# Hybrid decoder block: warm-up on a tile of ones, the last row's banks filled ahead, and new due times

## The chip, the cores and the metric

One NeuronCore of one Trainium2 chip. The kernel is one program on one core. Times are device microseconds of an execution; the time before is the median of 3 runs. The engines are named as in the profile: PE (TensorE matmuls), PEld (its weight loads), DVE (VectorE), ACT (ScalarE), POOL (GpSimd) and SP (SyncE, which here only issues transfers).

## The reference, cut to what matters

One layer of a decoder trunk on 512 positions of width 1024, in float32, with 97 MB of weights.

```python
h = rmsnorm(x) * g                                # 512 x 1024
proj = h @ w_in                                   # gated conv B, C, v | GLU a, b | queries | 3 gates
y_a = (B * conv3(C * v)) @ w_a_out
y_b = silu(layernorm(conv31(a * sigmoid(b)) + bias)) @ w_b_out
k, vm = split((rmsnorm(mem) * g_mem) @ w_kv)      # 256 memory tokens, 4 heads of 256
y_c = softmax(q k^T / 16) vm @ w_att_out
x = x + (sum of sigmoid(gate_i) * y_i) @ w_o
u = conv3(rmsnorm(x) @ w_up);  gt, up = split(u)  # 2 x 2816
x = x + (silu(gt) * up) @ w_down
return rmsnorm(x) * g_final
```

## The kernel before

**Arithmetic.** Every float32 product is made of three matmuls in a faster format: each operand is split into a high part (a cast, on ACT) and a low part (operand minus high part, on DVE), and high x high, high x low and low x high are added in one PSUM bank. So each weight unit of 128 x 1024 words is loaded by a transfer into `wf`, cast by ACT to `whi` (L638), subtracted by DVE to `wlo` (L642), and then used by 24 matmuls of 256 columns or 12 of 512. The large products are made by a scheme with seven in place of eight block products, which needs sums of blocks of the activations (made by DVE) and of the weights (mostly added by transfers that POOL issues, L762).

**Stages, in order of time.** The keys and values of the memory (`K`, `V`; matmuls at L1093 and, through the helper `product`, L589 to L591), the norm of x, the mixer's input products with the two convolutions and the attention between them (matmuls at L808), the three output products with their gates (L1580 to L1582), `w_o`, the FFN's up products (L808 again) with conv3 taps (L1536), gate product `z` (L1899) and its splits (`zh` L2086, `zl` L2093), and the down product by seven block products called a, b, d, c, f, e, g (L589 to L591 again). In the down product a, c, e and g follow each other in the same two banks ("chain e" is what a, c and e left there).

**Who sets the order.** PE's order is written out by hand (`seq`). All other work is a list of jobs with an engine, a cost, predecessors and places in buffers. `Jobs.run` plays them through with a small model: at each step it takes, over all engines, the job that can start first, and among those that can start at the same time the one with the smallest due. A due is counted back from PE's order, or is the place in the hand-written list `jobs.first` (15 names, places -15 to -1; they cover the first loads), and to it the table `LATER` adds a number for each kind of job. `AHEAD` says how long before its due a kind may start at the earliest; a kind that is not in it may start at once. A kind is the engine and the first words of the job's name (`SP ldm`: loads of the memory tiles). The resulting order is then fixed for each engine.

**The start.** `warm_up` (L1930) multiplies the identity matrix, which POOL builds (a fill and a select), 9 times with itself; float32 products run as two passes, so there are 18 rows. SP loads the memory's transposed tiles in halves of 256 KB (`ldm`, L906) and the first weights of K and V in halves (`ld0`, L1027). ACT makes `mh` (L916), DVE `ml` (L923), ACT and DVE make the halves of `whi` and `wlo` (L1036, L1040). PE's first product is K's first unit by halves (`K0`: 12 matmuls each), then V's first unit by halves (6 matmuls each), then V's second unit and so on.

**The end.** Product g adds to bank t = 0 of the chain for row block 2's left half, and for row block 3's left half it uses two banks of their own, 256 columns each (`end_banks`, `end_steps`), so that the last matmuls of each finish one after the other. Row block 3's left half is therefore its residual, plus what chain e left in bank t = 1 (`read_end(2)`, L2248, before g ends), plus the end banks (`read_end(0)` and `read_end(1)`, L2248, after their last matmul). Then ACT squares each half and sums it (L2251), takes the root (L2272), DVE the reciprocal (L2326), and DVE scales the left half in two parts (`last_scaled`, L2291), ACT the right half (`right_scaled`, L2278). Each part is stored at once: L2280, L2287 and L2294 on SP, the last right half on ACT's queue. Row blocks 0 to 2 go the same way, with L2284 for the left half.

Of the kernel before, what the change touches and what calls it, by code (L numbers as in the profile page):

```python
# [14 lines left out]
P = 128  # L15
# [62 lines left out]
    "ACT c3": 11.82, "ACT cf": -173.01, "ACT csq": -118.38, "ACT exp": -328.94,  # L78
# [3 lines left out]
    "ACT m root": -184.55, "ACT mgh a": -50.41, "ACT mgh b": 12.56, "ACT mgh c": 9.52,  # L82
    "ACT mgh d": 53.07, "ACT mgh e": -17.66, "ACT mgh f": 328.16, "ACT mgh g": -26.95,
    "ACT mh": 113.01, "ACT msq": -103.23, "ACT mu high": -95.05, "ACT oh": -89.08,
# [8 lines left out]
    "ACT sa": 32.95, "ACT sg": 5.87, "ACT sigmoid": 255.67, "ACT silu": -398.77,  # L93
    "ACT sq": -293.17, "ACT sr": -87.26, "ACT swish": -14.1, "ACT tap 0": 43.05,
    "ACT tap 1": 18.01, "ACT tap 2": -228.98, "ACT tap 3": 177.05, "ACT tp 0": -29.48,
# [9 lines left out]
    "ACT xroot": -102.97, "ACT xsq": -103.24, "ACT xsquare": 24.41, "ACT zh a": -216.1,  # L105
    "ACT zh b": -131.07, "ACT zh c": -165.28, "ACT zh d": -50.38, "ACT zh e": -12.01,
    "ACT zh f": -0.17, "ACT zh g": 24.3, "DVE CV": -0.26, "DVE c3": 18.44, "DVE centre": 14.23,
    "DVE cf": 2.06, "DVE csum": 176.43, "DVE ends": 101.48, "DVE fl h b00": -8.47,
# [4 lines left out]
    "DVE hd": -0.61, "DVE kl": -10.74, "DVE kt": 186.09, "DVE lns": -8.31, "DVE low": -452.45,  # L113
    "DVE m fold": -54.18, "DVE m scale": -85.77, "DVE mgl a": -80.95, "DVE mgl b": -52.58,
    "DVE mgl c": -276.12, "DVE mgl d": -6.76, "DVE mgl e": -420.56, "DVE mgl f": -72.56,
    "DVE mgl g": 51.17, "DVE ml": -3.7, "DVE ms c": -29.57, "DVE ms d": -655.28,
    "DVE ms e": -37.35, "DVE ms f": -0.78, "DVE msum": 27.5, "DVE mu fold": -21.28,
    "DVE mu low": -259.6, "DVE mu sum": -65.96, "DVE ol": -72.74, "DVE pn": -7.9,
    "DVE ptl": -14.54, "DVE ql": -83.03, "DVE r2 glu": 917.93, "DVE r2 up": 167.98,
# [5 lines left out]
    "DVE rl": -1.6, "DVE s6 glu": -90.48, "DVE sum": 19.99, "DVE sv": -29.87, "DVE tap 0": -45.34,  # L125
    "DVE tap 1": -70.16, "DVE tap 2": 353.84, "DVE tap 3": 43.8, "DVE top": -52.16,
    "DVE tot1": -14.34, "DVE tot2": 102.84, "DVE um": 102.16, "DVE v scale": -37.68,
    "DVE var fold": 7.3, "DVE var sum": 3.04, "DVE vl": 24.74, "DVE wl K 0": 49.62,
# [9 lines left out]
    "DVE x1 g": 14.24, "DVE xn": -647.51, "DVE xnorm": 196.37, "DVE xsum": -68.7,  # L138
    "DVE ymul": -34.71, "DVE ys": -1.41, "DVE z": -34.43, "DVE zd": 0.07, "DVE zl a": -144.78,
    "DVE zl b": -105.24, "DVE zl c": 218.14, "DVE zl d": 2.42, "DVE zl e": 85.69,  # L140
    "DVE zl f": 17.13, "DVE zl g": -3.75, "DVE zs c": 122.42, "DVE zs d": 21.17,
    "NONE c3": -263.88, "NONE cf": -131.91, "NONE mem tile": -34.72, "NONE raw tile K": 2.19,
    "NONE raw tile V": -2.93, "NONE rows": -101.12, "NONE sums": 33.35, "NONE temps": -19.31,
# [5 lines left out]
    "POOL s7 glu": -196.56, "POOL s7 up": -11.58, "POOL wadd e": 33.74, "POOL wadd x": -2.01,  # L149
    "POOL wadd y": 9.99, "POOL wl merge 0": -341.32, "POOL wl merge 2": 20.27, "POOL xa": -55.62,  # L150
# [308 lines left out]
def hybrid_block_kernel(  # L459
# [1466 lines left out]
    def warm_up():  # L1926

        ps = make(("bank", "warm"))
        for i in range(9):
            nc.tensor.matmul(ps[:, :P], ident, ident, start=True, stop=True)  # L1930
# [470 lines left out]
```

## Time and profile before

| | us |
|---|---|
| median of 3 runs | 897.81 (897.07 to 898.18) |
| the profiled execution | 897.59 |
| its span, first to last instruction | 895.8 |
| PE busy | 885.8 (99%) |
| DVE busy | 823.9 (92%) |
| ACT busy | 677.6 (76%) |

A row of the timeline gives the start and the length of an instruction in us, engine, line, operation, output <- inputs, shapes and count, and in brackets how long the engine idled before it and what ended that. A row of the chain of waits gives start, length and what the end of the program hung on. A row of the table by stretches gives the window, its length, then for PE, PEld, DVE, ACT and POOL the busy time (and instructions), then the granted PE clock, the mean busy share of the 16 DMA engines and GB/s. A matmul's row is longer than the distance to the next one, because matmuls overlap.

### The profile page before, as it was taken

The page shows a single profiled execution, that of the slowest core. Times are in us where ns is not written, and L with a number is a line of the kernel's source. Part 1 is how long each engine was busy: PE and PEld are TensorE (multiplying, and loading weights), DVE is VectorE, ACT ScalarE, POOL GpSimd, SP SyncE. Part 2 cuts the span into 40 slices and gives each one's busy share as a digit, 9 for nine tenths or more (in the row PEclk, how much of TensorE's full clock was granted, in tenths as well). Part 3 has the DMA queues.
Part 4 walks back from the last instruction along what each step waited for, and adds up shares of the span by engine and source line. Part 5 has one row for each costly group of instructions (what it writes and reads, how often), then busy time and mean ns, then how long its engine had stood idle before and what let it go on. Part 6 is the DMA issues. An engine that isn't in the chain of part 4 may idle for free.

```text
span 895.8 us, 16734 instructions
## 1 busy us (share of the span) xinstructions
PE 885.8 (99%) x6657; PEld 848.1 (95%) x6657; DVE 823.9 (92%) x929; ACT 677.6 (76%) x934; POOL 126.7 (14%) x153
## 2 busy tenths in 40 slices
PE   9999999999999999999999999999999999999997
PEld 8999999999989999999899988899999999988886
DVE  6997999999989999999978869898998889999997
ACT  7677989988988879778948743777776677866566
POOL 0011121101011121111100001021121121002120
PEclk9999999999999999999999999999999999999999
DMA  9998788757779889987858488599999878679992
GB/s 357 386 243 181 178 205 190 178 143 164 198 158 240 170 197 223 227 210 194 210 122 273 139 252 198 147 230 308 282 259 218 205 149 167 197 266 302 251 202 94
DMA packets 54366, 190.60 MB, mean 213 GB/s; under 512 B 6160, under 2 KB 6544, under 8 KB 54288
## 3 DMA queue, kind: packets, MB, share of 16 engines
q0 software_dynamic: 20880, 75.24, 46.3%
q1 hardware_dynamic: 33120, 114.02, 36.0%
q8 instruction: 52, 0.85, 0.4%
q10 hardware_dynamic: 288, 0.27, 0.1%
q14 instruction: 26, 0.21, 0.1%
HBM read 185.31 MB, written 4.19 MB: 212 GB/s over the span
## 4 chain that ended last, share of the span: by engine, by line
PE 94%; DVE 2%; ACT 1%; issue 1%; DMA 1%; SPq 0%; DVEq 0%
PE bank L808 60%; PE bank L590 6%; PE bank L591 6%; PE bank L589 6%; PE bank L1580 5%; PE bank L1581 5%; PE bank L1582 5%; PE bank L1093 2%; DVE wlo L642 1%; DMA mem<-in_mem_t 1%; PE bank L1819 0%; PE bank L1333 0%; ACT j L2251 0%; DVE upc L1536 0%; DVE gtc L1536 0%
## 5 line engine op out<-in xcount | busy, mean ns | idle before, releaser
L638 ACT CAST whi<-wf 128x1024 fp32r<-128x1024 f32 (+1 forms) x205 | 212.2, 1040 | 72.3 <-PE bank L808 35.1
L642 DVE TENSOR_TENSOR wlo<-wf,whi 128x1024 fp32r<-128x1024 f32 (+1 forms) x199 | 239.3, 1211 | 26.4 <-ACT whi L638 26.2
L1405 ACT ACTIVATE tp<-u,pk 128x511 f32<-128x511 f32 (+22 forms) x184 | 119.7, 707 | 5.7 <-DVE acc L1412 4.0
L1412 DVE TENSOR_TENSOR acc<-acc,tp 128x1020 f32<-128x1020 f32 (+22 forms) x92 | 109.2, 1189 | 5.6 <-ACT tp L1405 3.8
L762 POOL DMA_DIRECT2D wf<-in_w_in x56 | 49.5, 899 | 255.4 <-DVE wlo L642 170.0
L808 PE MATMUL bank<-ft6h,wlo 128*128 128x256 f32 x232 | 63.9, 275 | 0.7 <-DVE wlo L642 0.7
L808 PE MATMUL bank<-fb10h,whi 128*128 128x256 f32 x232 | 64.0, 276 | 0.0
L808 PE MATMUL bank<-fb11h,whi 128*128 128x256 f32 x232 | 64.0, 276 | 0.0
L808 PE MATMUL bank<-fb00h,whi 128*128 128x256 f32 x232 | 63.9, 275 | 0.0
L808 PE MATMUL bank<-fb00l,whi 128*128 128x256 f32 x232 | 63.8, 275 | 0.0
L808 PE MATMUL bank<-fb00h,wlo 128*128 128x256 f32 x232 | 63.8, 275 | 0.0
L808 PE MATMUL bank<-fb10l,whi 128*128 128x256 f32 x232 | 63.8, 275 | 0.0
L808 PE MATMUL bank<-fb10h,wlo 128*128 128x256 f32 x232 | 63.8, 275 | 0.0
L808 PE MATMUL bank<-ft5l,whi 128*128 128x256 f32 x232 | 63.8, 275 | 0.0
L808 PE MATMUL bank<-ft5h,wlo 128*128 128x256 f32 x232 | 63.8, 275 | 0.0
L808 PE MATMUL bank<-ft6l,whi 128*128 128x256 f32 x232 | 63.8, 275 | 0.0
L808 PE MATMUL bank<-ft7l,whi 128*128 128x256 f32 x232 | 63.8, 275 | 0.0
L808 PE MATMUL bank<-ft7h,wlo 128*128 128x256 f32 x232 | 63.8, 275 | 0.0
L808 PE MATMUL bank<-ft4l,whi 128*128 128x256 f32 x232 | 63.8, 275 | 0.0
L808 PE MATMUL bank<-ft4h,wlo 128*128 128x256 f32 x232 | 63.8, 275 | 0.0
L808 PE MATMUL bank<-fb11l,whi 128*128 128x256 f32 x232 | 63.8, 275 | 0.0
L808 PE MATMUL bank<-fb11h,wlo 128*128 128x256 f32 x232 | 63.8, 275 | 0.0
(381 smaller groups left out, 3143.1 us busy)
## 6 DMA issues: line engine op xcount, KB each, us to landing
wf<-in_w_in POOLq DMA_DIRECT2D x56, 512.0 KB, 6.8
wf<-in_w_in SPq DMA_DIRECT2D x54, 512.0 KB, 5.5
wf<-in_w_up POOLq DMA_DIRECT2D x33, 512.0 KB, 7.3
wf<-in_w_up SPq DMA_DIRECT2D x29, 512.0 KB, 6.8
wf<-in_w_down SPq DMA_DIRECT2D x15, 512.0 KB, 4.5
wf<-in_w_att_out SPq DMA_DIRECT2D x8, 512.0 KB, 3.6
wf<-in_w_a_out SPq DMA_DIRECT2D x8, 512.0 KB, 3.7
wf<-in_w_b_out SPq DMA_DIRECT2D x8, 512.0 KB, 4.6
```

Of the source, the lines that this page charges most:

```text
L589: nc.tensor.matmul(ps, s_hi, w_hi, start=start, stop=False, skip_group_check=again)
L590: nc.tensor.matmul(ps, s_hi, w_lo, start=False, stop=False, skip_group_check=again)
L591: nc.tensor.matmul(ps, s_lo, w_hi, start=False, stop=stop, skip_group_check=again)
L638: nc.scalar.copy(parts[0], src())
L642: nc.vector.tensor_tensor(lo, src(), hi.bitcast(F32), op=ALU.subtract)
L762: nc.gpsimd.dma_start(out=tiles[key], in_=block(w, col[c], k), accum_op=ALU.add)
L808: nc.tensor.matmul(ps[:, c, :], w[:, i, at], in_turns(a[i]), start=first and n == 0, stop=i == 3 and n == 2, skip_group_check=again,)
L1405: nc.scalar.activation(two(("tp", p, s))[:, j, s:], two(("u", p))[:, j, : SEQ - s], AF.Copy, scale=weight(j),)
L1412: nc.vector.tensor_tensor(a, a, two(("tp", p, s))[:, :, s:], op=ALU.add)
L1580: nc.tensor.matmul(ps, w_hi[:, i, at], hi, start=first, stop=False)
L1581: nc.tensor.matmul(ps, w_hi[:, i, at], lo, start=False, stop=False)
L1582: nc.tensor.matmul(ps, w_lo[:, i, at], hi, start=False, stop=last)
```

## The change

Three parts, in one edit.

- `warm_up` multiplies a tile of ones, which DVE fills, 11 times with itself; it waits for that fill and no longer for POOL's identity. In the first K unit the high x high matmuls of its first half (4 of the 12) become a PE job of their own, `K00`, ahead of the other 8. The second chunk of the first `mh` is made by DVE (`first_high`) and no longer by ACT.
- The end banks are filled by DVE before g starts: residual plus what chain e left in bank t = 1, in two adds of 256 columns. g's matmuls are added to that, with no starting flag. The adds after g are gone; ACT squares and DVE scales straight from the banks. g's first PE job waits for the fill.
- `LATER` and `AHEAD` are replaced as a whole (a few hundred numbers; the diff below shows the entries that the text names), and the kinds `sa`, `sv`, `sq`, `hd`, `sr`, `rt` and `rc` of the last rows now have a number for each row block.

```diff
 LATER = {
...
-    "SP ldm": -808.23, "SP ld0 K": -1347.82, "SP ld0 V": -250.98, "SP ld V 0": -0.13,
+    "SP ldm": 1.07, "SP ld0 K": -59.18, "SP ld0 V": 0.74, "SP ld V 0": -0.51,
-    "ACT sa": 32.95, "ACT rt": -228.68, "DVE z": -34.43, "DVE cf": 2.06,
+    "ACT sa 0": -186.83, "ACT rt 1": -69.87, "ACT rt 2": -135.8, "DVE z": 26.85, "DVE cf": 235.06,
...
 }
...
-        elif key[0] in ("tap", "tp"):
+        elif key[0] in ("tap", "tp", "sa", "sv", "sq", "hd", "sr", "rt", "rc"):
             words = key[:2]
...
-                for i in range(2 * e, 2 * e + 2):
+                for i in range(2 * e, 2 * e + (1 if g == e == 0 else 2)):
                     nc.scalar.activation(
                         tiles["mh", g][:, i, :], four(("mem", g))[:, i, :], AF.Copy,
                         scale=par("norm_mem_g", 4 * g + i),
                     )
+
+            def first_high():
+                memory_parts(0)
+                nc.vector.tensor_scalar(
+                    tiles["mh", 0][:, 1, :], four(("mem", 0))[:, 1, :], par("norm_mem_g", 1), None,
+                    op0=ALU.mult,
+                )
...
+            pe(("K00",), 4 * MM_QUAD, lambda: keys_product(0, 0, (0, 1), (0,)),
+               [("wh0", "K", 0), ("mh", 0, 0), "mh1"], take=[(bank, "ps")], unit=False)
             for e in range(2):
-                pe(K0 if e else ("K0",), 12 * MM_QUAD,
-                   lambda e=e: keys_product(0, 0, (2 * e, 2 * e + 1)), [("wl0", "K", e), ("ml", 0, e)],
-                   take=[] if e else [(bank, "ps")], use=[bank] if e else [], unit=e == 1)
+                pe(K0 if e else ("K0",), (12 if e else 8) * MM_QUAD,
+                   lambda e=e: keys_product(
+                       0, 0, (2 * e, 2 * e + 1), (0, 1, 2) if e else (1, 2)),
+                   [("wl0", "K", e), ("ml", 0, e)], use=[bank], unit=e == 1)
...
         ps = make(("bank", "warm"))
-        for i in range(9):
-            nc.tensor.matmul(ps[:, :P], ident, ident, start=True, stop=True)
+        w = tiles["ones",][:, :P]
+        for i in range(11):
+            nc.tensor.matmul(ps[:, :P], w, w, start=True, stop=True)
+
+    def ones():
+        nc.vector.memset(make(("ones",))[:, :P], 1.0)
...
         if p == "g":
-            banks = banks[:1] + (end_banks if u == 1 else [])
+            banks = banks[:1] + (end_banks if u < 2 else [])
+            needs += [("rd", "end")] if u == 0 else []
...
                 product(
-                    ps[:, :256], hi[:, k % 2, cols], lo[:, k % 2, cols],
+                    end_bank(i), hi[:, k % 2, cols], lo[:, k % 2, cols],
                     four(("zh", "g", k // 4))[at], four(("zl", "g", k // 4))[at],
-                    k == 0, k == PAIRS - 1,
+                    False, k == PAIRS - 1, again=True,
                 )
...
-    def read_end(i):
-        row = late["x1"][NT - 1][0]
-        src = tiles["bank", chain("e"), 1]
-        if i < 2:
-            row, src = row[:, ENDS[i]], tiles[end_banks[i]][:, :256]
-        nc.vector.tensor_tensor(parted(row), parted(row), turned(src), op=ALU.add)
+    def read_end():
+        row, src = late["x1"][NT - 1][0], turned(tiles["bank", chain("e"), 1])
+        for i in range(2):
+            make(end_banks[i])
+            nc.vector.tensor_tensor(
+                turned(end_bank(i)), parted(row[:, ENDS[i]]), parted(src[:, i, :]), op=ALU.add)
...
+    def square_end(i, into):
+        nc.scalar.activation(late["junk"][0][:, ENDS[i]], end_bank(i), AF.Square, accum_out=into)
...
         nc.vector.scalar_tensor_tensor(
-            x1, x1, r_fin[NT - 1], late["g"][0][:, cols], op0=ALU.mult, op1=ALU.mult
+            parted(x1), turned(end_bank(i)), r_fin[NT - 1], parted(late["g"][0][:, cols]),
+            op0=ALU.mult, op1=ALU.mult,
         )
...
             job(("sr", t, 1), "ACT", 0.4, lambda: square_end(1, ss_fin[last][:, 0:1]),
                 [("pd", "g", "rest", 1)], use=[end_banks[1]])
```

More of the change, by code (lines that the diff above doesn't have):

```diff
@@ L140 @@
[L140 to L143, printed above, removed]
[5 rows of a table removed]
-    "POOL s7 glu": -196.56, "POOL s7 up": -11.58, "POOL wadd e": 33.74, "POOL wadd x": -2.01,
-    "POOL wadd y": 9.99, "POOL wl merge 0": -341.32, "POOL wl merge 2": 20.27, "POOL xa": -55.62,
[7 rows of a table removed]
+    "ACT c3": -1.33, "ACT cf": -332.1, "ACT csq": 6.48, "ACT exp": 144.98, "ACT fh h b00": 1.04,
[3 rows of a table added]
@@ L158 @@
+    "DVE zl b": -133.2, "DVE zl c": -1.95, "DVE zl d": -57.09, "DVE zl e": -106.84,
+    "DVE zl g": -287.13, "DVE zs c": 331.9, "DVE zs d": -188.27, "DVE zs e": 198.82,
+    "NONE c3": -197.54, "NONE cf": 11.65, "NONE mem tile": -0.5, "NONE raw tile K": 4.49,
+    "NONE raw tile V": -1.04, "NONE sums": 3.7, "NONE temps": -26.39, "POOL ea": 5.97,
[6 rows of a table added]
+    "POOL wadd x": -92.48, "POOL wadd y": -265.13, "POOL wl merge 0": 0.31,
[7 rows of a table added]
 }
 AHEAD = {
-    "ACT cf": 41.7, "ACT csq": 1.4, "ACT exp": 30.8, "ACT fh h b00": 29.2, "ACT fh h b11": 14,
@@ L181 @@
-    "DVE mu fold": 8.3, "DVE mu low": 21.4, "DVE ol": 1.5, "DVE pn": 13.5, "DVE ptl": 1.9,
-    "DVE ql": 1.6, "DVE r3 cv": 6.6, "DVE r3 gate": 25.2, "DVE r3 q": 3.4, "DVE r7 bb": 29.2,
-    "DVE r7 cv": 5.7, "DVE r7 gate": 1.6, "DVE r7 glu": 1.6, "DVE rd c": 26.3, "DVE rd e": 18.2,
-    "DVE rd end": 12.8, "DVE rd f": 60, "DVE rl": 2.8, "DVE s6 glu": 1.2, "DVE tot1": 1.7,
-    "DVE var sum": 120.3, "DVE vl": 1.3, "DVE wl V 0": 114.3, "DVE wl merge 1": 17.6,
[7 rows of a table removed]
-    "NONE cf": 3.5, "NONE mem tile": 2.7, "NONE raw tile K": 39.9, "NONE raw tile V": 1.4,
@@ new lines @@
+    "ACT r1 gate": 34.5, "ACT r1 q": 1.5, "ACT r2 gate": 8.3, "ACT r2 glu": 53.1,
[4 rows of a table added]
+    "ACT sa 0": 1.7, "ACT sa 1": 49, "ACT sg": 1.7, "ACT sigmoid": 44.7, "ACT silu": 1.5,
+    "ACT sq 3": 51.6, "ACT sr 1": 5.2, "ACT sr 2": 3.8, "ACT swish": 86.3, "ACT tap 0": 135,
+    "ACT tap 1": 3.6, "ACT tap 3": 1.3, "ACT v root": 74.6, "ACT vh": 1.5, "ACT wh K 0": 5,
[4 rows of a table added]
+    "ACT zh a": 4.8, "ACT zh d": 17.5, "ACT zh g": 3.3, "DVE csum": 10.8, "DVE ends": 9.1,
[3 rows of a table added]
+    "DVE kl": 42.8, "DVE kt": 52.5, "DVE low": 2.8, "DVE m fold": 3, "DVE m scale": 5.4,
@@ L204 @@
+    "DVE zl a": 65.2, "DVE zl d": 8, "DVE zl e": 85.2, "DVE zl f": 37.3, "DVE zl g": 22.2,
+    "NONE c3": 1.1, "NONE cf": 41.5, "NONE mem tile": 8.1, "NONE raw tile K": 1.9,
+    "NONE raw tile V": 2.5, "NONE rows": 3.9, "NONE sums": 45.8, "POOL s3 cv": 7.1,
[8 rows of a table added]
 }
@@ L901, in hybrid_block_kernel, with memory_parts @@
     R_MEM, R_X, R_V, SS_X, ATT = column(0, MC), column(2, NT), column(60, NT), 6, 12
+    def memory_parts(g):
+        for part, side in (("mh", "h"), ("ml", "l")):
+            if (part, g) not in tiles:
+                tiles[part, g] = forms.tile(
+                    [P, 4, HALF], F32R, tag=MEM_PLACE[g] + side, name=name(part))
     for g in range(2):
@@ L911, in mem_high @@
                 if e == 0:
[L912 to L915 removed]
+                    memory_parts(g)
+                for i in range(2 * e, 2 * e + (1 if g == e == 0 else 2)):
                     nc.scalar.activation(
@@ L1928, in warm_up @@
         ps = make(("bank", "warm"))
-        for i in range(9):
-            nc.tensor.matmul(ps[:, :P], ident, ident, start=True, stop=True)
-    pe(("warm",), 4.9, warm_up, take=[(("bank", "warm"), "ps")], unit=False)
+        w = tiles["ones",][:, :P]
[3 more added lines that the diff above has]
+        nc.vector.memset(make(("ones",))[:, :P], 1.0)
+    job("ones", "DVE", 0.2, ones, take=[(("ones",), ANY)])
+    pe(("warm",), 4.75, warm_up, ["ones"], take=[(("bank", "warm"), "ps")], use=[("ones",)],
+       unit=False)
     KEYS = lambda h, g: lambda: pe_keys(h, g)
@@ L2010, in pe_down @@
         pe(("pd", p, u), n, lambda: steps(p, (u,), ts), needs,
-           take=[(k, "ps") for k in (banks if new else end_banks if (p, u) == ("g", 0) else [])],
+           take=[(k, "ps") for k in (banks if new else [])],
            use=[("zh", p, u // 2), ("zl", p, u // 2)] + ([] if new else banks))
@@ L2299, in hybrid_block_kernel @@
             if p == "g" and t:
-                job(("rd", "end", 2), "DVE", dve(512), lambda: read_end(2),
-                    [("pd", "e", NU - 1)] + rows_in, use=[("bank", chain("e"), t)])
-                for i in range(2):
-                    job(("rd", "end", i), "DVE", dve(256), lambda i=i: read_end(i),
-                        [("pd", "g", "rest", i), ("rd", "end", 2)], use=[end_banks[i]])
+                job(("rd", "end"), "DVE", 2 * dve(256), read_end,
+                    [("pd", "e", NU - 1)] + rows_in, take=[(k, "ps=whole") for k in end_banks],
+                    use=[("bank", chain("e"), t)])
             else:
```

101 lines of the change are left out of this document (53 added, 48 removed), and 155 rows, old and new, of tables (AHEAD, LATER).

## The prediction

> **What bounds the kernel now.** I read the page first, then TensorE's (PE's) list of waits, the chain of waits at the start, the rows of PE around each gap in the timeline, and the table by stretches.
>
> ```profile
> PE 885.8 (99%) x6657; PEld 848.1 (95%) x6657; DVE 823.9 (92%) x929; ACT 677.6 (76%) x934; POOL 126.7 (14%) x153
> ```
> ```profile
> PE bank L808 <- DVE wlo L642: 0.7, 1, 0.7
> PE bank L591 <- DVE zl L2093: 0.4, 1, 0.4
> ```
> PE is busy 99% of 895.8 us, and the change takes no matmul of the computation away. So it can win in three places only: before PE runs without a break, in PE's gaps, and after the last matmul. All three are small.
>
> The start, from the chain of waits:
>
> ```profile
> 2.12 5.08 DMA mem<-in_mem_t
> ...
> 7.22 2.51 ACT mh L916 x6
> 9.73 0.52 ACT whi L1036
> ...
> 10.27 0.70 DVE wlo L1040
> ...
> 11.49 0.22 PE bank L591
> ```
> The kernel starts on a transfer: the second half of the first memory tile lands at 2.12 + 5.08 = 7.20. Then ACT scales six memory chunks in a row, and only then makes the high part of V's first weights (from 9.73). DVE follows with the low part until 10.97. What PE does meanwhile:
>
> ```profile
> 1.36 4.21 PE L1930 MATMUL bank<-ident 128*128 128x128 f32 x18 [1.36 <-POOL ident masks.py:199]
> 5.26 0.58 PE L1093 MATMUL bank<-mh,whi 128*128 128x256 f32 x1
> ...
> 8.37 0.38 PE L1093 MATMUL bank<-ml,whi 128*128 128x256 f32 x1 [0.17 <-DVE ml L923]
> ...
> 9.54 0.28 PE L1093 MATMUL bank<-ml,whi 128*128 128x256 f32 x1
> 9.65 0.28 PE L1093 MATMUL bank<-mh,wlo 128*128 128x256 f32 x1
> 10.29 0.48 PE L589 MATMUL bank<-whi,mh 128*128 128x512 f32 x1 [0.37 <-ACT whi L1036]
> 11.01 0.48 PE L590 MATMUL bank<-wlo,mh 128*128 128x512 f32 x1 [0.24 <-DVE wlo L1040]
> ```
> A 256-column product follows the one before it after 0.11 us (9.54 to 9.65), a 512-column one after 0.22 (the chain's row at 11.49). So PE could have gone on at 9.76 and did at 10.29 (0.53 lost), and at 10.51 and did at 11.01 (0.50 lost): **1.03 us stand before V's first half, none of it PE's own speed**.
>
> The gaps in the middle:
>
> ```profile
> 620.93 0.28 PE L808 MATMUL bank<-ft6l,whi 128*128 128x256 f32 x1
> 621.89 0.38 PE L808 MATMUL bank<-ft6h,wlo 128*128 128x256 f32 x1 [0.69 <-DVE wlo L642]
> ...
> 805.85 0.38 PE L591 MATMUL bank<-whi,zl 128*128 128x512 f32 x1
> ...
> 807.51 0.48 PE L591 MATMUL bank<-whi,zl 128*128 128x512 f32 x1 [0.38 <-DVE zl L2093]
> ```
> From start to start, 0.96 - 0.11 = 0.85 is lost at 621. At 806 three products lie between the two rows, 1.66 - 3 x 0.22 = 1.0. The list of waits shows less, because the rows of neighbouring matmuls overlap.
>
> The end:
>
> ```profile
> 887.04 0.48 ACT L2272 ACTIVATE cols<-cols 128x1 f32<-128x1 f32 x2
> 887.57 0.72 ACT L2278 ACTIVATE x<-x,cols 128x512 f32<-128x512 f32 x1
> 888.60 1.32 ACT L2278 ACTIVATE x<-x,cols 128x512 f32<-128x512 f32 x2
> 888.90 0.28 PE L591 MATMUL bank<-whi,zl 128*128 128x256 f32 x1
> 889.29 0.41 DVE L2248 TENSOR_TENSOR x<-x,bank 128x256 f32<-128x256 f32 x1
> 889.82 0.40 ACT L2251 ACTIVATE j<-x 128x256 f32<-128x256 f32 x1
> ```
> ```profile
> 890.00:894.00 4.00, 0.00 (x0) 0.00 (x0) 1.49 (x4) 1.33 (x4) 0.00 (x0) 0.70 1.05 403
> 894.00:895.00 1.00, 0.00 (x0) 0.00 (x0) 0.00 (x0) 0.00 (x0) 0.00 (x0) 0.50 0.43 150
> ```
> The last matmul ends at 889.18, DVE adds until 889.70, ACT squares from 889.82. Two things stand beside that chain. ACT is not free any earlier: its scaling of rows 1 and 2 runs from 888.60 to 889.92 (rows overlap by 0.1). And the DMA share, the last but one number, is 1.05 from 890 to 894 at 403 GB/s and 0.43 in the next: the output keeps the transfers full until about 894.4.
>
> **The change part by part.** The profiled execution took 897.59, its span 895.8, so 1.8 lie around the span; the median of the three runs is 897.81, 0.22 above it. I sum differences and put them on the median.
>
> *Ones.* DVE fills 128x128 where GpSimd built the identity, so PE starts near 1.0 (an estimate; at worst at 1.36 as now). Eleven products are 22 passes of (5.26 - 1.36)/18 = 0.217: 4.77 us, until 5.8. That is 0.5 later than the first product now. What covers it is the memory half that lands at 7.20: PE waits for its low part until 8.37 anyway, and 12 products of 0.21, the last ones faster as now, bring it there near 8.0. Cost 0; without the cover 0.5.
>
> *First product early.* Four high-by-high matmuls run before the low parts are there, and DVE makes one chunk that ACT made.
>
> ```profile
> 4.33 0.89 DVE L923 SCALAR_TENSOR_TENSOR ml<-mem,pk,mh 128x256 fp32r<-128x256 f32 x2 [4.33 <-ACT mh L916]
> ```
> DVE idles until 4.33, and one 128x256 operation of it takes about 0.45 (0.89 for two): 0, at worst 0.45. The matmuls are the same 24, and what they gain ends again at the memory half: 0.
>
> *Order of the first loads.* This comes from the two tables alone, and is where I expect the gain of the start. Before, SP's dues fall by 808 for the memory loads and by 251 for V's halves, so all four memory halves go ahead of V:
>
> ```profile
> 2.12 1.38 SPq L906 DMA_DIRECT2D mem<-in_mem_t  x3
> 3.54 0.91 SPq L1027 DMA_DIRECT2D wf<-in_w_v  x2
> ...
> 9.63 1.12 ACT L1036 CAST whi<-wf 128x512 fp32r<-128x512 f32 x2
> ```
> ```profile
> wf<-in_w_v SPq DMA_DIRECT2D x2, 256.0 KB, 5.7
> ```
> In the new tables the terms are +1.07 and +0.74, so the places in the list decide (-9 for the first memory tile's second half, -7 and -6 for V's halves, -3 and -2 for the second memory tile). V's first half moves from seventh to fifth. It is then issued at 2.12 + 0.46 = 2.58 and lands 5.1 (the memory load) to 5.7 later, by 8.3 in place of 9.2. ACT splits it by 8.9 (0.56 each), DVE by 9.6, before PE asks at 9.76. Both gaps close: -1.03. V's second half stays the eighth 256 KB, lands near 9.7, and is split by 11.0 to 11.5 where PE asks for it at 11.28: up to 0.2 is given back, 0.8 if a whole unit is split ahead of it. I take **-0.87**; ends -1.03 and 0 (the order of issue is not what I read). The gain has to last through the stage after it:
>
> ```profile
> 12.00:60.00 48.00, 48.00 (x348) 45.36 (x347) 46.83 (x58) 33.96 (x40) 5.35 (x6) 1.00 0.98 342
> ```
> DVE (the third busy figure) has 48.00 - 46.83 = 1.17 idle there, more than 0.87, so it can.
>
> *Dues in the middle.* Every due changes, and with it the order on ACT, DVE, SP's queue and GpSimd's. The wait at 621 comes from one choice: DVE took the gate product before the low part that PE needed.
>
> ```profile
> 619.48 1.23 DVE L1899 TENSOR_TENSOR z<-upc,gtc 128x1024 f32<-128x1024 f32 x1
> 620.62 1.22 DVE L642 TENSOR_TENSOR wlo<-wf,whi 128x1024 fp32r<-128x1024 f32 x1
> ```
> The product's due rises from -34 to +27, so it loses such a tie: **-0.85**. The wait at 806 hangs on the last conv block and a DVE that is full there (below): 0. New gaps are not in this trace; by the two that are, they lie between 0 and 2, and I take 0.
>
> *End banks.* DVE puts the residual plus what chain e left into the two banks, and g's matmuls are added to it. One add becomes two of 256:
>
> ```profile
> 873.01 0.68 DVE L2248 TENSOR_TENSOR x<-x,bank 128x512 f32<-128x512 f32 x1
> ...
> 874.52 0.27 PE L589 MATMUL bank<-whi,zh 128*128 128x256 f32 x1
> ```
> The 256 form took 0.41 (889.29), so 0.82 for 0.68. But now all of g on PE queues behind it. In the same place it ends at 873.83, 0.69 ahead: 0; one 1.22 weight split put ahead of it costs 0.5. After the last matmul the add (0.41 and 0.1 of handing over) goes: up to -0.5. What is late next is ACT, busy to 889.92, so little of that shows. In the new dues row 0's scaling (-187) passes the roots of rows 1 and 2 (-70, -136), so output starts up to 0.48 earlier than 888.29 and the full queue drains by 893.9 in place of 894.4; the last store is issued no earlier. I take **-0.2**; ends -1.0 (ACT free at 889.3, and the earlier start) and +0.4 (half of one more 0.72 scaling in the way).
>
> Here a rule can be weighed. The last two stores land late:
>
> ```profile
> DMA to landing us min/median/max: 2.6/2.9/3.1
> ```
> The Trainium skill, DMA: Bandwidth & Descriptors, section "Anatomy of one DMA — SWDGE (gpsimd) path", gives a transfer a fixed 2.0 us or so, mostly the receipt, plus its bytes over 436 GB/s. That would be 2.3 for 128 KB, so by the rule alone the queue ahead is worth up to 0.8, and the sum would come to 895.3, inside the forecast's own range below. By the trace the queue is full and moves 0.48 at most.
>
> *Sum:* 0 + 0 - 0.87 - 0.85 + 0 - 0.2 = -1.92: 897.81 - 1.92 = **895.9**.
>
> **The rivals.**
>
> *Given back.* The new order leaves PE as much in the middle as the old, 1.85 us in other places. Then the first and last terms stay: 897.81 - 1.07 = 896.7. For it: DVE was busy 98% from 12 to 60, so an earlier PE meets the same DVE. Against: the wait at 621 is one tie. That the change doesn't do what it says goes with this one: if V's halves are not issued earlier, warm-up and early product do nothing for the time, and -0.85 - 0.2 is again 896.8.
>
> *All gaps close.* The 1.0 at 806 goes too, and the end reaches its -1.0: 895.9 - 1.0 - 0.8 = 894.1. Against: DVE has no idle time there.
>
> *DVE late in the down projection: slower.* Its place is 780 to 869:
>
> ```profile
> 780.00:869.00 89.00, 88.47 (x444) 77.87 (x443) 87.82 (x94) 56.28 (x65) 15.75 (x18) 1.00 0.93 255
> ```
> DVE has 89.00 - 87.82 = 1.2 spare. The new dues push the conv taps of the FFN back (+2 becomes +235). One side of one block is four taps and the gate product:
>
> ```profile
> L1536 DVE SCALAR_TENSOR_TENSOR gtc<-gt,pk,gtc 128x510 f32<-128x510 f32 x22 | 16.5, 750 | 0.7
> ```
> 4 x 0.75 + 1.22 = 4.2 us. If that enters late, PE waits 4.2 - 1.2 = 3.0: 897.81 + 3.0 - 0.87 = 899.9. It decides from 1.2 us of deferred work on, and the kernel is slower than before from about 2.1. Against: a job starts as soon as DVE is free, so a due only settles ties.
>
> **How the numbers follow.** A measurement of this kernel can tell 0.2%, 1.8 us, from no change; the line is 896.0. The forecast has a chance of 0.42, with its own range from 894.9 to 896.9, two thirds of it under the line; 896.7 has 0.23; 894.1 has 0.11; 899.9 has 0.24. Faster is 0.28 + 0.11 = 0.39, same 0.14 + 0.23 = 0.37, slower 0.24. The range is 894.0 to 900.1: about half of the fast rival and half of the slow one lie outside.
>
> **What would show it.** V's first load as fifth on SP, its split done by 9.7 and PE's first 512-column product near 9.8; no wait near 621 in PE's list; the adds into the end banks done by 874; ACT's last square near 889.8 less what PE gained, so no nearer to the last matmul although the add is gone, with the DMA share at 1 up to the end. The prediction is wrong if the square follows the last matmul within 0.15 and the end moves with it, if PE's first V product still waits for ACT, or if PE's list holds new waits over 2 us, first of all for low parts between 780 and 869.

## The result, and the profile after

| | before | after |
|---|---|---|
| median, us | 897.62 (8 runs, 896.75 to 898.18) | 899.63 (8 runs, 898.77 to 900.71) |
| the profiled execution, its span | 897.59, 895.8 | 898.77, 896.8 |

The changed kernel is **slower by 0.25%**, 2.0 us: the ratio is 1.0025, interval 1.0014 to 1.0036. The forecast was 895.9, faster by 0.2%. The time lies within the range on record, on the other side of the forecast. The profiled execution of the changed kernel is the quickest of its eight, so its profile shows less than the whole difference.

The page first. The busy times stand where they were:

```profile
PE 885.6 (99%) x6661; PEld 847.5 (95%) x6661; DVE 823.8 (92%) x930; ACT 677.4 (76%) x933; POOL 127.0 (14%) x153
```

No engine has more to do, so the loss is waiting. PE's list of waits (total, times, longest):

```profile
PE bank L592 <- DVE x L1814: 0.9, 1, 0.9
PE bank L811 <- ACT gt L840: 0.9, 1, 0.9
PE bank L593 <- DVE wlo L1057: 0.9, 1, 0.9
PE bank L592 <- ACT zh L2114: 0.4, 1, 0.4
PE bank L594 <- DVE zl L2121: 0.4, 1, 0.4
```

The `zl` row, at 806, was there before with the same 0.4; PE waited 0.7 at the place of the L811 row too, but for a low part of DVE. The first and the fourth row are new. The third had a row of its kind (0.2, for V's first half); this one is for the second half. Row by row, with the timeline of the changed kernel around each.

**The start.** SP's issues, ACT, DVE and PE:

```profile
2.60 0.43 SPq L1044 DMA_DIRECT2D wf<-in_w_v  x1
8.39 1.04 ACT L641 CAST whi<-wf 128x1024 fp32r<-128x1024 f32 x1 [0.73 <-DMA wf<-in_w_v]
9.34 0.61 ACT L1053 CAST whi<-wf 128x512 fp32r<-128x512 f32 x1
10.61 0.68 DVE L1057 TENSOR_TENSOR wlo<-wf,whi 128x512 fp32r<-128x512 f32 x1
8.55 0.38 PE L592 MATMUL bank<-whi,mh 128*128 128x512 f32 x1
10.01 0.48 PE L592 MATMUL bank<-whi,mh 128*128 128x512 f32 x1
11.35 0.48 PE L593 MATMUL bank<-wlo,mh 128*128 128x512 f32 x1 [0.86 <-DVE wlo L1057]
```

V's first half is the fifth load, as read from the tables, and PE starts on it at 8.55 instead of 10.29. Then PE waits for the second half: from 10.01 to 11.35, 1.12 more than the pace. ACT split a whole unit (8.39) ahead of it.

**571.** DVE before and after:

```profile
569.53 1.29 DVE L1811 SCALAR_TENSOR_TENSOR xnorm<-x,cols,gffn 128x1024 f32<-128x1024 f32 x1
570.84 0.69 DVE L1793 TENSOR_TENSOR x<-x,bank 128x512 f32<-128x512 f32 x1
```
```profile
569.65 1.28 DVE L1832 SCALAR_TENSOR_TENSOR xnorm<-x,cols,gffn 128x1024 f32<-128x1024 f32 x1
571.04 1.28 DVE L1832 SCALAR_TENSOR_TENSOR xnorm<-x,cols,gffn 128x1024 f32<-128x1024 f32 x1
572.25 1.28 DVE L1814 TENSOR_TENSOR x<-x,bank 128x512 f32<-128x512 f32 x2
571.08 1.06 PE L1840 MATMUL bank<-ident,xnorm 128*128 128x128 f32 x8
573.07 0.45 PE L592 MATMUL bank<-whi,mgh 128*128 128x512 f32 x1 [0.93 <-DVE x L1814]
```

The add of chain e into x1, for whose bank the next product of w_o waits, came right behind the first norm. Now the second norm (1.28) stands ahead of it. PE makes eight transposes here and then goes on with that product, 0.79 after the first transpose in the kernel before (571.93 to 572.72), and 573.07 - 571.08 = 1.99 after it now: 1.2 lost.

**621 and 806.** The gate product (`z`) still goes ahead of the low part that PE needs, and ACT now splits a late weight unit ahead of the read that PE needs:

```profile
620.15 1.22 DVE L1920 TENSOR_TENSOR z<-upc,gtc 128x1024 f32<-128x1024 f32 x1
620.85 1.06 ACT L641 CAST whi<-wf 128x1024 fp32r<-128x1024 f32 x1 [0.60 <-DMA wf<-in_w_up]
621.26 0.28 PE L811 MATMUL bank<-ft7h,wlo 128*128 128x256 f32 x1
622.44 0.38 PE L811 MATMUL bank<-ft6h,whi 128*128 128x256 f32 x1 [0.91 <-ACT gt L840]
804.12 1.22 DVE L645 TENSOR_TENSOR wlo<-wf,whi 128x1024 fp32r<-128x1024 f32 x1
805.26 1.22 DVE L1920 TENSOR_TENSOR z<-upc,gtc 128x1024 f32<-128x1024 f32 x1
806.62 0.38 PE L594 MATMUL bank<-whi,zl 128*128 128x512 f32 x1
807.39 0.48 PE L592 MATMUL bank<-whi,zh 128*128 128x512 f32 x1 [0.40 <-ACT zh L2114]
808.53 0.48 PE L594 MATMUL bank<-whi,zl 128*128 128x512 f32 x1 [0.39 <-DVE zl L2121]
```

1.18 - 0.11 = 1.07 at 621 (0.85 before). From 806.62 to 808.53 four rows stand three paces of 0.22 apart: 1.91 - 0.65 = 1.26 lost (1.0 before).

**The end.**

```profile
889.30 1.32 ACT L2310 ACTIVATE x<-x,cols 128x512 f32<-128x512 f32 x2
889.93 0.28 PE L594 MATMUL bank<-whi,zl 128*128 128x256 f32 x1
890.53 0.37 ACT L2286 ACTIVATE j<-bank 128x256 f32<-128x256 f32 x1
```
```profile
891.00:894.00 3.00, 0.00 (x0) 0.00 (x0) 1.32 (x4) 1.01 (x2) 0.00 (x0) 0.75 1.05 405
895.00:896.00 1.00, 0.00 (x0) 0.00 (x0) 0.00 (x0) 0.00 (x0) 0.00 (x0) 0.50 0.39 135
```
```profile
DMA to landing us min/median/max: 3.1/3.2/3.4
```

The add is gone, and the square starts 0.60 after the last matmul does (0.92 before), held by ACT's two scalings. The last line is the time from issue to landing of the last two stores, 2.6 to 3.1 before: they are issued earlier after the last matmul (the first of them 892.27 - 889.93 = 2.34 for 891.39 - 888.90 = 2.49), and land later after their issue. The transfers are full from 891 until about 895.4. From the start of the last matmul to the end of the span it is 896.8 - 889.93 = 6.87, and before 895.8 - 888.90 = 6.90.

### The profile page after: what moved, and what is told of

Its sections match the earlier page's. It is cut to its first block, busy times and chain, and to the rows that moved or that the text cites. A ratio compares the mean times of both kernels' runs of the same rounds, so it can differ in the third digit from the quotient of the medians.

```text
span 896.8 us, 16700 instructions
## 1 busy us (share of the span) xinstructions
PE 885.6 (99%) x6661; PEld 847.5 (95%) x6661; DVE 823.8 (92%) x930; ACT 677.4 (76%) x933; POOL 127.0 (14%) x153
## 4 chain that ended last, share of the span: by engine, by line
PE 90%; DMA 3%; DVE 3%; ACT 1%; issue 1%; SPq 1%; DVEq 0%; ACTq 0%
PE bank L811 56%; PE bank L594 6%; PE bank L593 6%; PE bank L592 6%; PE bank L1601 5%; PE bank L1603 5%; PE bank L1602 5%; DMA wf<-in_w_up 3%; PE bank L1111 2%; DVE wlo L645 1%; DMA wf<-in_w_kv 1%; ACT whi L641 0%; PE bank L1354 0%; DVE x L2264 0%; DVE zl L2121 0%
## 5 line engine op out<-in xcount | busy, mean ns | idle before, releaser
L641 ACT CAST whi<-wf 128x1024 fp32r<-128x1024 f32 x196 | 202.6, 1039 | 58.1 <-PE bank L811 20.1
L645 DVE TENSOR_TENSOR wlo<-wf,whi 128x1024 fp32r<-128x1024 f32 (+1 forms) x190 | 228.5, 1211 | 16.8 <-ACT whi L641 16.3
L1426 ACT ACTIVATE tp<-u,pk 128x510 f32<-128x510 f32 (+22 forms) x184 | 119.4, 703 | 4.0 <-DVE acc L1433 3.8
L765 POOL DMA_DIRECT2D wf<-in_w_in x45 | 40.3, 911 | 190.8 <-DVE wlo L645 141.5
L811 PE MATMUL bank<-ft6h,whi 128*128 128x256 f32 x232 | 63.9, 275 | 0.9 <-ACT gt L840 0.9
L811 PE MATMUL bank<-fb10h,whi 128*128 128x256 f32 x232 | 64.0, 276 | 0.0
L811 PE MATMUL bank<-fb11h,whi 128*128 128x256 f32 x232 | 64.0, 276 | 0.0
L811 PE MATMUL bank<-ft5l,whi 128*128 128x256 f32 x232 | 63.9, 275 | 0.0
L811 PE MATMUL bank<-fb00h,whi 128*128 128x256 f32 x232 | 63.9, 275 | 0.0
L811 PE MATMUL bank<-fb00l,whi 128*128 128x256 f32 x232 | 63.9, 275 | 0.0
L811 PE MATMUL bank<-fb00h,wlo 128*128 128x256 f32 x232 | 63.8, 275 | 0.0
L811 PE MATMUL bank<-fb10l,whi 128*128 128x256 f32 x232 | 63.8, 275 | 0.0
L811 PE MATMUL bank<-fb10h,wlo 128*128 128x256 f32 x232 | 63.8, 275 | 0.0
L811 PE MATMUL bank<-ft5h,wlo 128*128 128x256 f32 x232 | 63.8, 275 | 0.0
L811 PE MATMUL bank<-ft6l,whi 128*128 128x256 f32 x232 | 63.8, 275 | 0.0
L811 PE MATMUL bank<-ft6h,wlo 128*128 128x256 f32 x232 | 63.8, 275 | 0.0
L811 PE MATMUL bank<-ft7l,whi 128*128 128x256 f32 x232 | 63.8, 275 | 0.0
L811 PE MATMUL bank<-ft7h,wlo 128*128 128x256 f32 x232 | 63.8, 275 | 0.0
L811 PE MATMUL bank<-ft4l,whi 128*128 128x256 f32 x232 | 63.8, 275 | 0.0
L811 PE MATMUL bank<-ft4h,wlo 128*128 128x256 f32 x232 | 63.8, 275 | 0.0
L811 PE MATMUL bank<-fb11l,whi 128*128 128x256 f32 x232 | 63.8, 275 | 0.0
```

Source lines behind the costliest of these rows:

```text
L641: nc.scalar.copy(parts[0], src())
L645: nc.vector.tensor_tensor(lo, src(), hi.bitcast(F32), op=ALU.subtract)
L765: nc.gpsimd.dma_start(out=tiles[key], in_=block(w, col[c], k), accum_op=ALU.add)
L811: nc.tensor.matmul(ps[:, c, :], w[:, i, at], in_turns(a[i]), start=first and n == 0, stop=i == 3 and n == 2, skip_group_check=again,)
L1426: nc.scalar.activation(two(("tp", p, s))[:, j, s:], two(("u", p))[:, j, : SEQ - s], AF.Copy, scale=weight(j),)
```

## The experiments

Two rows cut each span in three: PE's first product with w_in, and its last matmul. For the kernel before, a second profile of it, and the changed kernel:

```profile
41.94 0.27 PE L808 MATMUL bank<-fb00h,whi 128*128 128x256 f32 x1
```
```profile
41.00 0.27 PE L808 MATMUL bank<-fb00h,whi 128*128 128x256 f32 x1
887.79 0.28 PE L591 MATMUL bank<-whi,zl 128*128 128x256 f32 x1
```
```profile
40.88 0.27 PE L811 MATMUL bank<-fb00h,whi 128*128 128x256 f32 x1
```

The same two rows of all profiles ("start" is where PE reaches w_in, "middle" from there to the last matmul, "end" from there to the end of the span), with medians and ratios. Each ratio is against the runs of the kernel before beside it, whose medians were 897.24 to 897.89; e8 to e11 ran on another chip than the rest, so their times compare with the others by the ratios only.

| kernel | start | middle | end | median | ratio, interval |
|---|---|---|---|---|---|
| before | 41.94 | 846.96 | 6.90 | 897.62 | |
| before, again | 41.00 | 846.79 | 6.91 | one run: 896.48 | |
| e1 code, old dues | 41.04 | 847.06 | 6.90 | 896.97 | 1.0000, 0.9991 to 1.0009 |
| e3 old middle | 40.91 | 847.21 | 6.88 | 897.42 | 1.0003, 0.9994 to 1.0012 |
| changed | 40.88 | 849.05 | 6.87 | 899.63 | 1.0025, 1.0014 to 1.0036 |
| e0 changed again | 41.20 | 849.96 | 6.84 | 899.46 | 1.0027, 1.0018 to 1.0037 |
| e4 571 moved | 41.86 | 848.79 | 6.85 | 898.65 | 1.0016, 1.0007 to 1.0025 |
| e5 621 moved | 41.08 | 849.18 | 6.84 | 899.69 | 1.0030, 1.0017 to 1.0042 |
| e6 806 moved | 41.72 | 848.13 | 6.85 | 899.21 | 1.0022, 1.0013 to 1.0031 |
| e7 all three | 41.26 | 848.02 | 6.82 | 897.90 | 1.0009, 1.0000 to 1.0018 |
| e8 halves first | 42.07 | 848.71 | 6.82 | 900.26 | 1.0034, 1.0022 to 1.0046 |
| e9 left store first | 41.23 | 848.58 | 6.79 | 899.43 | 1.0022, 1.0014 to 1.0031 |
| e10 e1 + 806 moved | 41.81 | 846.92 | 6.87 | 896.55 | 0.9991, 0.9982 to 1.0000 |
| e11 e3 + two moves | 41.66 | 847.37 | 6.87 | 898.01 | 1.0010, 1.0001 to 1.0019 |
| e12 e10 + one move | 41.56 | 846.68 | 6.86 | 896.77 | 0.9988, 0.9979 to 0.9997 |

My theory: the new dues cost the middle, by the place of single jobs on DVE and ACT; the edits of the code are worth nothing. Rivals: the end banks' fill or the start on ones costs it; or transfers that land late here and there.

**Where it is: e0, e1, e3, b1.** e0 is the changed kernel as it is, b1 the kernel before. e1 has all edits of the code and the dues of before; e3 has those dues only for jobs due between 60 and 860:

```diff
+self.new[key] = kind in ("DVE ones", "DVE mh1") or not 60 < due[key] < 860   # e1: or False
-due[key] += LATER.get(self.kind(key), 0.0)
+due[key] += LATER.get(kind, 0.0) if self.new[key] else LATER0.get(self.old_kind(kind), 0.0)
```

> The changed kernel once more, as it is. Both theories: 899.6, 0.25% above the kernel before. What is asked is which of PE's gaps in the middle come back in a second profile. Theory of the dues: 571 (1.27), 621 (1.1 to 1.2) and 806 to 808 (1.36) are all there again, and what this run is longer than the 898.8 of the first profile stands in the gap at 621, which ends a chain that began on a transfer (landing 13.9 after its issue). Rival (noise of transfers everywhere): other places appear.

> All edits of the code (ones, first product early, end banks), but every due from the tables of before; the kinds that are now one per row have the old kind's value. Theory of the dues (the loss is the new order in the middle, the edits of the code are worth nothing): 897.6, ratio 0.9990 to 1.0010, PE's gaps those of before (621: 0.85, 806: 1.0), V's first product again near 10.3. Rival (the end banks' add, on which all of g now waits, or the start on ones costs the time): 898.5 to 899.6, with a wait of PE on the end banks' add near 874 or a first product later than 5.26.

> The changed kernel with the dues of before for every job whose due by PE's clock lies between 60 and 860; start and end keep the new dues. Theory of the dues: the start keeps its 0.9, the middle has the two gaps of before, the end is worth 0: 897.6 - 0.9 = 896.7, ratio 0.999. Rival (given back: whatever PE gains at the start meets a DVE that is full, whatever the dues): 897.6, with new gaps of 0.9 in all before 500. Rival (the end costs): 898 or more.

> The kernel before, once more, for a second look at its start. In its first profile the second memory half landed at 7.20 and PE reached the first product of w_in's first unit at 41.94; with the same order of loads and the edited code the half landed near 6.1. If the landing of the first loads varies from one execution to the next, the half lands between 6.0 and 6.6 here and PE reaches w_in near 41.0 to 41.5, and the 0.9 that I credited to the order of the loads is mostly such a draw. If it is the order (or the start on the identity), it is 7.1 to 7.3 and 41.9 again.

e1 runs as the kernel before does (to within 0.09% either way, 0.8 us), so the code is worth nothing that can be told. The middle is 846.8 to 847.2 with the old dues in four profiles (mean 847.0), and 848.6 to 850.0 with the new ones in the five that leave it as it is (changed, e0, e5, e8, e9; mean 849.1): **2.1 us, all of the loss**. By medians in one set of runs, putting back the middle's dues alone takes 899.46 to 897.42. e3 was to come out at 896.7 and did not: the start's 0.9 is missing. b1 shows why. In it and in e1 the old order of loads has PE at w_in by 41.0, as early as the new one; with the new one it is 40.9 to 41.9 in the eight that have it unmoved (changed, e0, e3 to e7, e9). The mean is 41.47 over the five profiles with the old order and 41.27 over these eight. What moved between the two profiles of the kernel before is the landing. ACT's scaling of the second memory half, in b1 (7.22 in the first profile, with SP's issue of that half at 2.12 in both):

```profile
6.01 2.11 ACT L916 ACTIVATE mh<-mem,pk 128x256 fp32r<-128x256 f32 x5
```

e0's gaps are those at 571 (1.2), 621 (1.2, half of it on DVE's low part now) and 806 (1.3). PE's order is the same in all kernels, so the middle can be cut further, at rows that all profiles have. From the eight transposes at 571 to the first product of the FFN:

```profile
571.93 1.04 PE L1819 MATMUL bank<-ident,xnorm 128*128 128x128 f32 x8
578.86 0.27 PE L808 MATMUL bank<-fb00h,whi 128*128 128x256 f32 x1
```
```profile
579.20 0.27 PE L811 MATMUL bank<-fb00h,whi 128*128 128x256 f32 x1
```

That is 6.93 before and 579.20 - 571.08 = 8.12 after. It is 6.93 or 6.94 in all seven profiles with the old dues in the middle, and 8.12 in all six that have the new ones and leave this place as it is. Another 0.16 is lost just ahead of the transposes. So 1.35 of the 2.1 stand at 571. The stretch at 806 is 0.26 longer, the one from 579 to 605 by 0.2 to 0.4. The wait at 621 is another matter: PE's list has 0.9 there in the first profile of the changed kernel, 0.4 twice in e0, 0.2 in e8 and nothing in e9, with the same order of these jobs in all four. With the old dues it has 0.7 and 0.3 in the two profiles of the kernel before, and 0.4 twice in e10. The second profile of the kernel before, and e8:

```profile
PE bank L808 <- DVE wlo L642: 0.3, 1, 0.3
```
```profile
PE bank L823 <- ACT gt L852: 0.2, 1, 0.2
```

So its size is mostly a draw of the execution, with either order.

e0 also loses 0.2 at 614, and ahead of it ACT stood 2.07 for a transfer:

```profile
612.18 2.00 ACT L641 CAST whi<-wf 128x1024 fp32r<-128x1024 f32 x2 [2.07 <-DMA wf<-in_w_up]
```

A late transfer may be part of that 0.2, but such a wait is not peculiar to the new dues: e3 has one of 2.07 too, at 609, and PE loses nothing behind it. The new dues do leave the transfers idler at 560 to 580; before and after (the last but one number is the share):

```profile
560.00:580.00 20.00, 20.00 (x108) 17.75 (x107) 17.68 (x23) 14.88 (x22) 0.86 (x1) 1.00 0.52 136
```
```profile
560.00:580.00 20.00, 19.07 (x100) 16.47 (x99) 16.89 (x22) 13.63 (x22) 1.73 (x2) 1.00 0.29 78
```

From 580 to 620 the share is 1.01 before and 1.03 after. No run here tries that part by itself.

**Which places: e4 to e7.** The planner's result stays, and one job is emitted behind another:

```diff
+HOLD = {("xnorm", 1): ("x1", "e", 0)}                  # e4
+HOLD = {("wh", (("up", 1), 4)): ("r1", ("up", 2))}     # e5
+HOLD = {("wl", ("pd", "b", 3)): ("zl", "a", 2)}        # e6; e7 has all three
-            fn()
+            if key in HOLD:
+                self.held.setdefault(HOLD[key], []).append(fn)
+            else:
+                fn()
...
+            for late in self.held.pop(key, ()):
+                late()
```

> The changed kernel with one job moved: on DVE the second half of the FFN's norm (row 1) goes behind the first add of chain e into x1, as in the kernel before; nothing else changes its place. Theory of the dues: the gap at 571 shrinks from 1.27 to 0.1, and since nothing else moves, the time falls by 1.1, to 898.5. Rival (a DVE that is full only hands the wait on): the gap goes and another of the same size comes within 40 us, 899.6.

> The changed kernel with one job moved on ACT: the high part that waits for a late transfer (up block 1, unit 4) goes behind the read of the gate bank for which PE waits at 621, as in the kernel before. Theory one (ACT's order makes the whole gap): the gap at 621 goes, 899.5 - 1.0 = 898.5. Theory two (DVE's low part of unit 6 of block 2, made after the gate product, is ready only 0.1 to 0.3 us earlier than the read): the wait is handed from ACT to that low part, 0.2 is gained, 899.3.

> The changed kernel with one job moved on DVE near 804: the low part of w_down's unit 3 of chain b (1.22 us) goes behind the low part of the last gate product, so that the product of the last conv block (z) starts at 804.15 in place of 805.26. Theory (PE's 1.36 at 806 to 808 is this one place in DVE's order): the gap falls by 1.1 to 0.2 or so, 899.5 - 1.1 = 898.4. Rival (ACT's high part of z, or DVE again at the low part of unit 3, ends last anyway): a new wait on that low part near 809, 899.2 to 899.5.

> The changed kernel with the three moves (571, 621, 806) together. Theory (three waits, each its own): the sum of the single ones, 0.8 (measured at 571) + 0.2 to 1.0 + 1.1 = 2.1 to 2.9, so 896.6 to 897.4, on the kernel before or under it. Rival (a full DVE hands on what it gains): less than 1.5 of it, 898 or more.

e4: the product of g follows the transposes without a wait, and 0.8 of the 1.2 comes back, in the time (899.46 to 898.65) and in the stretch from the transposes to the FFN (8.12 to 7.36):

```profile
572.42 1.06 PE L1851 MATMUL bank<-ident,xnorm 128*128 128x128 f32 x8
573.24 0.46 PE L603 MATMUL bank<-whi,mgh 128*128 128x512 f32 x1
```

The rest went into small gaps behind it, at 574 (0.4) and 580 (0.3). e5 gains nothing (899.69). The wait passes from ACT's read to DVE's low part, as theory two said:

```profile
621.71 0.28 PE L822 MATMUL bank<-ft6l,whi 128*128 128x256 f32 x1
623.00 0.38 PE L822 MATMUL bank<-ft6h,wlo 128*128 128x256 f32 x1 [1.02 <-DVE wlo L656]
```

e6: the gap at 806 falls from 1.26 to 0.33 (from 807.33 to 807.88, less a pace), and a new one of 0.37 comes before 818.50. By medians it gains 0.25 (899.46 to 899.21), no more than can be told, and the time is what the rival said:

```profile
807.33 0.38 PE L604 MATMUL bank<-wlo,zh 128*128 128x512 f32 x1
807.88 0.48 PE L605 MATMUL bank<-whi,zl 128*128 128x512 f32 x1 [0.17 <-DVE zl L2132]
817.91 0.38 PE L603 MATMUL bank<-whi,zh 128*128 128x512 f32 x1
818.50 0.48 PE L604 MATMUL bank<-wlo,zh 128*128 128x512 f32 x1 [0.21 <-DVE wlo L656]
```

e7 gains 1.6 against e0, less than the 2.1 to 2.9 of the sum, and its interval just reaches the kernel before (1.0000). So the place at 571 is shown, by the two runs that move it and by the stretch above; 621 is not ACT's alone; and a gap taken away at a full DVE comes back in part.

**Start and end: e8, e9.**

```diff
+HOLD = {("wh", ("V", 0, 1)): ("wh0", "V", 1), ("wl", ("V", 0, 1)): ("wl0", "V", 1)}   # e8
-    "DVE sv 0": 2.06                                                                     # e9
+    "DVE sv 0": -60
```

> The changed kernel with two jobs moved at the start: the high and the low part of V's first whole unit go behind those of V's second half, for which PE waits 0.86 in every profile of the changed kernel. Theory (the order of the first loads is worth 0.9, but the whole unit that is split ahead of the second half takes it back): the wait near 10.3 falls to 0.2 or less, PE reaches w_in's first product near 40.5 (40.9 to 41.9 so far, in both kernels), and the time falls by 0.8, to 898.7. Rival (the second half lands no earlier than it is split now): the wait stays at 0.8, the time at 899.5.

> The changed kernel with one due: DVE scales row 0's left half as soon as its factor is there, so that its store is issued about 0.9 us earlier, and the last row's chain about 0.3 later by the planner's costs. From the start of the last matmul to the end it is 6.82 to 6.91 in all ten profiles, of both kernels. Theory (the full transfers set the end): the 0.5 us of idle transfer time at 889 to 891 is used, 6.3 to 6.5, the time 0.4 less, 899.1. Rival (the last row's chain of square, root and scaling sets it): 7.1 to 7.2, the time 0.3 more, 899.8.

e8: the wait for the second half is gone, but nothing is won (1.0034, against 1.0027 for e0); the half itself lands late, and PE is at w_in at 42.07:

```profile
9.79 0.62 ACT L1065 CAST whi<-wf 128x512 fp32r<-128x512 f32 x1 [1.13 <-DMA wf<-in_w_v]
```

In these profiles the start goes mostly by when the loads land, and neither the order of issue nor that of splitting shows through. In e9 the transfers were emptier at 895 (0.16 for 0.39), the issue of the last stores came 0.2 later from the last matmul, and the end is 6.79, for 6.87 in the first profile and 6.82 in e8, beside it on the same chip. What the later issue cost, the shorter landing gave back:

```profile
DMA to landing us min/median/max: 2.3/2.6/2.9
```

**Is there a quicker one: e10 to e12.** e10 is e1 with e6's move, e11 is e3 with the moves of e6 and e8, e12 is e10 with one more:

```diff
+HOLD = {("wl", ("pd", "b", 3)): ("zl", "a", 2), ("zs", "c", 2): ("wl", ("pd", "d", 3))}   # e12
```

> The edited code with all dues of before, and the one move on DVE near 804 (low part of w_down's unit 3 of chain b behind the low part of the last gate product). Theory (PE's 1.1 at 805 to 807 is this place): 897.2 - 0.7 = 896.5, under the kernel before; from w_in's first product to the last matmul 846.3 or less where the four profiles with old dues have 846.8 to 847.2. Rival: 847.0 and 897.2, the wait only moves on.

> New dues at the start and the end, dues of before in the middle, V's halves split ahead of the whole unit, and the move near 804. If both single moves are worth what the theory says (0.8 at the start, 0.7 at 806): 897.4 - 1.5 = 895.9, the quickest of all. If only the one at 806 is: 896.7. If neither: 897.4.

> As the kernel with all dues of before and the one move near 804, and a second move on DVE behind it: one scaled copy of the gate product for a later chain (0.96 us at 813) goes behind four weight splits of chain d. In the profile with the first move alone the wait at 806 fell from 1.1 to 0.2, but PE, now earlier, waited 0.47 for a low part of chain d at 817. Theory (each wait is one place in DVE's order, and the second move frees the second place): no wait at 817, the middle 0.5 shorter than with the first move, 896.1, ratio 0.9985. Rival (DVE is full, and each move only hands the wait on): a new wait of 0.3 to 0.5 between 817 and 860, 896.6.

e10 comes out near what was expected in time, with the middle 846.92 and not 846.3: its own 621 was wider (1.2) in that profile. The stretch at 806 is 0.9 shorter, and 0.5 of that is lost again at 817. e11 missed: 898.01, slower than e10 by 1.5, though its middle is only 0.45 longer; the new dues of start and end are no gain there either. The two kernels that change tables at 60, e3 and e11, lose 0.4 and 0.6 between w_in's first product and 162 that e1 and e10 do not, which may be the seam and not the dues. e12 has no wait at 817 and another of the same size (0.59 - 0.22 = 0.37) at 836, as the rival said:

```profile
835.83 0.38 PE L751 MATMUL bank<-whi,zh 128*128 128x512 f32 x1
836.42 0.48 PE L752 MATMUL bank<-wlo,zh 128*128 128x512 f32 x1 [0.21 <-DVE wlo L804]
```

At 0.9988 (0.9979 to 0.9997) e12 has the lowest ratio of all: the edited code, the old dues, two jobs moved. It cannot be told from e10 (0.9991), so the second move shows no gain; and as the lowest of twelve kernels, with an interval that ends at 0.9997, its 0.12% under the kernel before is not a sure one.

## Why the prediction was wrong, point by point

- **Dues in the middle, -0.85: the step that failed.** It took one wait away by comparing one due with another (the gate product at 621), and priced all new gaps at 0. The wait at 621 stayed (1.07 in the first profile, 1.2 in the second), since the gate product still came first. By the planner's code a due settles only between jobs that can start at the same time, and holds back only the kinds in `AHEAD`, where the new table no longer has this product. On the chip it was no tie: by the order of the rows, the high part that the low part is made from was ready at 619.55 before, and DVE began the product at 619.48 (620.25 and 620.15 after). And the 0.85 was one draw of a wait that the kernel before has at 0.5 in its second profile. The new gaps are the larger part: 1.35 at 571, where the second norm passed the add, 0.26 at 806 and 0.2 to 0.4 from 579 to 605. Measured +2.1 for the whole term. The bounds written beside it for new gaps, 0 to 2, were about the right size; the value taken was the wrong end.
- **Order of the first loads, -0.87: failed too.** The mechanism happened as read (V fifth, PE at 8.55), and the profile even showed PE 1.06 earlier at w_in. But the kernel before is there by 41.00 as well in its second profile. The 1.03 of gaps did not decide it: e1 has both (0.59 and 0.51) and is at w_in at 41.04. What the new order gains on V's first half is lost on the second (1.12), the case that I had priced at 0.8 and not taken. Measured about 0, or 0.2 by the means of the starts, less than they scatter; by medians the new dues of start and end give +0.45 (e3 against e1), less than these runs can tell.
- **Ones and First product early, 0:** right as far as can be told, e1 at 1.0000 with 0.0009 either way. PE started on the ones at 1.06.
- **End banks, 0, and the end, -0.2:** no wait on the fill shows in PE's list. The end moved by 0.03 to 0.06, and in e1, with the old dues, by nothing (6.90). That ACT is late next and the transfers stay full was right. That the square would come no nearer to the last matmul was not: it came 0.32 nearer. The gain was mis-sized. Of the output only the first store starts earlier (1.24 before the last matmul for 0.58), the second does not (0.02 for 0.15). The share is 0.47 and 0.44 in the us from 889 and from 890, for 0 and 0.87 from 888 and from 889 before, so the transfers are done no sooner, and the last stores land late behind them.
- **The rivals.** The slower one named low parts between 780 and 869. It came out slower, by 2.0, but not there: from 780 to 869 only the 0.26 at 806 is new, and two thirds of the loss stand at 571, ahead of the FFN and its conv taps. That its 899.9 lies 0.3 from the 899.63 measured is luck, and so is that the range, whose upper end came from this rival, holds the time. "Given back" had the start surviving and the middle unchanged, and neither held.
- **The rule on stores.** By the rule of the Trainium skill, DMA: Bandwidth & Descriptors, section "Anatomy of one DMA — SWDGE (gpsimd) path", a transfer costs a fixed part and its bytes. The Trainium skill gives it there for transfers that GpSimd issues, and these stores are issued by SP and ACT. By it alone the sum stood at 895.3. The trace does not agree: the last stores took 3.1 to 3.4 behind the full queue, not the 2.3 that it gives for 128 KB, and the end gained 0.03 to 0.06. In e9, with the queue shorter, they took 2.3 to 2.9.

Open is what the idler transfers at 560 to 580 cost: e7's three moves leave 1.0 of the middle's loss, all of it between 570 and 605, and no run tells there how much is late transfers and how much the order on DVE. Open is also why the plan put the second norm ahead of the add at 571.

## What to carry to other kernels

When a whole order is replaced around engines that are 76 to 99% busy, price new gaps at the size of the old ones: nothing says that a new order has fewer. Cut the span at rows that both kernels have, and look at two profiles of the kernel before, before a gap is counted as something to win: here the start moved by 0.9 and the wait at 621 from 0.7 to 0.3 between two of them. A wait that one move takes away beside a full engine is worth what is left after the next wait, here from nothing to 0.8 of 1.2.

## What the runs showed of the hardware that was not expected

The first loads land at different times in executions of the same program: in the two profiles of the kernel before, SP issues the second memory half at 2.12, ACT's scaling of it starts at 7.22 and 6.01, and PE reaches w_in at 41.94 and 41.00. Over all 15 profiles, of 13 kernels, the issue is at 2.11 to 2.13, the scaling between 6.00 and 7.26, and w_in between 40.88 and 42.07. That half is not all of it: in e4 its scaling starts at 6.17, and PE is at w_in at 41.86. The end is the opposite: 6.79 to 6.91 from the last matmul in every one of them. So about 1 us of the spread between these executions is made before PE reaches w_in.
